# A hybrid encoder on one core: another opening, bias-first adaLN sums and another order of the mixers

## The chip, the core and the metric

The kernel runs on one of the eight cores of a Trainium2 chip. The metric is the device time of one execution in microseconds (us); the time given is the median of a few runs. Names in the profile: PE is TensorE (PEld its weight loads), DVE is VectorE, ACT is ScalarE, POOL is GpSimd, SP is the engine whose queue issues nearly all DMA transfers.

## The reference

Two layers on x (1 x 256 x 1024, float32), with a vector c (1024) that modulates both sub-layers (adaLN):

```python
c_act = silu(c)
for l in range(2):
    sh1, sc1, gt1, sh2, sc2, gt2 = split(c_act @ w_ada[l] + b_ada[l], 6)
    h = rms(x, g_mix[l]) * (1.0 + sc1) + sh1
    parts = split(h @ w_in[l], ...)          # q, k, v of A; q, k, v of three groups B; two gates
    y_a = gqa_attention(rope(rms(qa)), rope(rms(ka)), va) @ w_branch_a[l]
    y_b = dilated_attention(...) @ w_branch_b[l]      # windows (128,1), (512,4), (2048,16)
    x = x + gt1 * ((sigmoid(gate_a) * y_a + sigmoid(gate_b) * y_b) @ w_out[l])
    h2 = rms(x, g_mlp[l]) * (1.0 + sc2) + sh2
    x = x + gt2 * (square(relu(h2 @ w_ff1[l])) @ w_ff2[l])
```

## The kernel before

The 256 tokens are two tiles (t = 0, 1) of 128 partitions. Products with weights run on TensorE in three passes of a 32-bit format: a weight tile (128 x 1024, one DMA of 512 KB into one of seven buffers `wr`) is split into a high part `w[:, 0]` by ScalarE and the rest `w[:, 1]` by VectorE, and the activations hT likewise; hi x hi, lo x hi and hi x lo are summed in PSUM.

**adaLN.** c_act is broadcast to all partitions. Each of 96 tiles of w_ada is loaded through a `wr` buffer too, and VectorE multiplies it with c_act and sums along the row in one instruction (`ada_tile`; CUSTOM_DVE in the profile). Its output is one column of `shg` (shift and scale) or `gcol` (gate). The bias `b_col` and the gain `g_col` come in afterwards: `first_sh_sc` for the first mixer, one k tile at a time, `sh_sc` for the three other norms, `gt_row` for the gates.

**The opening** is written out by hand in a table `OPEN`. `loads` is the order of the first DMAs on SP's queue, behind that of c: x0 (the first token tile, with an identity of 128 columns, biases, gains and rotary constants in front, 1552 columns), x1 (1280 columns), two tiles of w_ada, then w_x and w_y of k tile 0. `steps` is the order in which the work is recorded: C is the tanh of c and the products that broadcast it (`step_c`, 128 rows of c_in of which 8 hold c), T0 and T1 the first rotary table by products on 64 rows, X0 and X1 the mean square, rstd (GpSimd, a power of -0.5), scaling, transposes by the identity and copies to xT (`step_x`), A the two reduces that give shift and scale of k tile 0 (`step_a`), H0 and H1 h = xT * scale + shift (`step_h`), W the split of the weights, M the first products, F a few products that only keep the array busy. `eng` names the engine of each step (a is ScalarE, d VectorE). The products with w_y of k tile 0 are plain float32 (`plain`). Then come k tiles 1 to 7 of the first projections, 24 products each, each with two w_ada tiles and two weight tiles of its own.

**The order.** Everything is recorded in a `Plan` before it is issued. The planner runs the recorded work against its own table of costs, picks for each engine the next instruction by due time and by what is ready, and then issues all in the order that comes out. `seq0` and `seq1` give the order in which the pieces of the two mixers are recorded (a and b are pieces of the two attentions, c2 to c5 chunks of q, k, v, u and v gate products, y the A branch, w one w_ada tile), `ada_f0` how many w_ada tiles stand between the MLP's pieces. In the trace all recorded instructions carry one line, 721, of `issue`.

The attention uses the array divided: `ka,qa` on 64 rows, `qk` in 64 x 64, `pTa,v` and `pTb,v` in 64 columns; all else uses 128 x 128.

Of the kernel before, what the change touches and what calls it, by code (L numbers as in the profile page):

```python
# [12 lines left out]
F32 = mybir.dt.float32  # L13
# [7 lines left out]
P = 128  # L21
D = 1024
# [14 lines left out]
  ada_f0=[2, 3, 11, 2, 0, 1, 0, 8, 1], ada_f1=[1, 0, 0, 0, 0, 0, 0, 0, 0],  # L37
  seq0="w v v w a w c3 c4 a w w v w a v u a w w w w w u w w w b w b w w v w u w y w w w y w y y w".split(),
  seq1="w u w c4 v w w w w w a w u w c3 w v a a w c5 w w u w w c2 w a w y w y y w y w w u w b w w w b v w v w".split())
# [7 lines left out]
FIRST = 500.0  # L47
# [6 lines left out]
X0 = 128 + 16 + 128 + 256  # L54
OPEN = dict(
    loads="x0 x1 a0 a1 wx wy",
    steps="C T1 F0 X0 A X1 T0 F1 Wy H0 Wx H1 My0 Mx0 Mx1 My1",
    eng=dict(c0="a", c1="a", ss00="d", ss01="a", ss10="d", ss11="a", xn00="a", xn01="d", xn10="a",
             xn11="a", xT00="a", xT01="a", xT10="d", xT11="a", t00="a", t01="a", t10="a", t11="a",
             h0="d", h1="a", i0="d", i1="a"),  # L60
# [96 lines left out]
class Plan:  # L157
# [101 lines left out]
    def record(self, e, op, a, k):  # L259
        outs = [k["out"]] if "out" in k else [a[0]]  # L260
        outs += [z for z in (k.get("accum_out"),) if z is not None]
        ins = [z for z in list(a if "out" in k else a[1:]) + [v for n, v in k.items() if n not in ("out", "accum_out")] if pattern(z) is not None]
        if op == "tensor_tensor_reduce":
            outs.append(ins.pop())
        o = dict(e=e, op=op, a=a, k=k, w=[self.foot(z) for z in outs], r=[self.foot(z) for z in ins], i=len(self.ops))
        o["also"], o["then"], o["soon"] = [], None, self.soon and e == "SP"
# [22 lines left out]
    def cost(e, op, outs, ins, k):  # L289
# [18 lines left out]
        if e == "SP":  # L308
# [26 lines left out]
    def links(self):  # L335
        last = {}
        for o in self.ops:
            need = {}

            def wait(j, how, o=o, need=need):  # L340
                if j != o["i"]:
                    need[j] = max(need.get(j, 0), how)

            for kind, fs in (("r", o["r"]), ("w", o["w"])):
                for name, space, p0, p1, m in fs:
                    for j, jk, q0, q1, jm in last.get(name, ()):
# [7 lines left out]
                        late = not same or o["e"] == "SP" or (o["e"] != "PE" and kind == "r")  # L354
# [46 lines left out]
    def due(self, seq, at=None):  # L401
# [12 lines left out]
        for o in reversed(self.ops):  # L414
            i = o["i"]
            d = due[i]
            lat = 3500 if o["e"] == "SP" else o["lat"]
# [12 lines left out]
    def run(self, due):  # L430
# [8 lines left out]
        free["SP"] = 0.0  # L439
        pipe = [0.0]  # L440
        dve_port, held_port, last_cut = 0.0, (0.0, 0.0), ""
        chain, pending = False, None
# [34 lines left out]
        def expect(i, depth=0):  # L477
            z = 0.0
            for j, how in ops[i]["need"].items():
                if ops[j]["e"] == "SP":  # L480
                    z = max(z, landed.get(j, 1e18))
                    continue
# [63 lines left out]
        while count < n:  # L546
            moved = False
            for e in ORDERED:
# [15 lines left out]
                if pick is None and seen[e] == state[0] and e not in again:  # L564
                    if e == "DVE" and pending is not None:
# [70 lines left out]
                if e == "DVE":  # L636
# [4 lines left out]
                    chain = o["port"] and slow == 0.0 and "reduce" not in o["op"]  # L641
                elif e == "POOL":
                    if dve_port > t + 70.0:
                        late = True
                    elif o["port"]:
                        held_port = t, t + 70.0 + 2.14 * (o["occ"] - 140.0) / 2.16
# [78 lines left out]
def encoder(ctx: ExitStack, tc: tile.TileContext, a: dict, out: bass.AP):  # L725
# [23 lines left out]

    xin = cp.tile([P, X0 + 2 * D + 256], F32, name="xin")  # L750
    x = xin[:, X0 : X0 + 2 * D].rearrange("p (t d) -> p t d", t=2)
    ident, small, gc = xin[:, :P], xin[:, P : 2 * P], xin[:, 2 * P : 2 * P + 8]
    cs_of = xin[:, 2 * P + 16 : X0], xin[:, X0 + 2 * D :]
# [17 lines left out]
    def ada_tile(l, w, s, k, col):  # L771
# [5 lines left out]
        dve.tensor_tensor_reduce(junk, raw, c_act, 0.5, 0.0, ALU.mult, ALU.add, col)  # L777

    def sh_sc(l, w, k0, k1):

        v = shg[l, w]
        dve.tensor_tensor(v[:, :, k0:k1], v[:, :, k0:k1], b_col[:, l, w, 0:2, k0:k1], op=ALU.add)
        dve.scalar_tensor_tensor(
            v[:, 1, k0:k1], v[:, 1, k0:k1], 1.0, g_col[:, l, w, k0:k1], op0=ALU.add, op1=ALU.mult
        )

    def first_sh_sc(k):

        v, gb = shg[0, 0], b_col[:, 0, 0, 1, :]
        if k == 0:  # L790
            dve.scalar_tensor_tensor(gb, gb, 1.0, g_col[:, 0, 0, :], op0=ALU.add, op1=ALU.mult)
        sc, sh = v[:, 1, k : k + 1], v[:, 0, k : k + 1]
        dve.tensor_scalar(sc, sc, g_col[:, 0, 0, k : k + 1], gb[:, k : k + 1], op0=ALU.mult, op1=ALU.add)
        dve.tensor_tensor(sh, sh, b_col[:, 0, 0, 0, k : k + 1], op=ALU.add)
# [795 lines left out]
    with plan.first():  # L1590
        sp.dma_start(c_in, a["c"])
# [41 lines left out]
    def step_c():  # L1633
# [106 lines left out]
    for k in range(1, KT):  # L1740
# [16 lines left out]
        if k == KT - 1:  # L1757
            with plan.not_before(62000.0):
# [65 lines left out]
def _layout(i):  # L1824
# [6 lines left out]
    r["c"] = con(np.concatenate([c, np.zeros((P - KT, P + KT), np.float32)], 0))  # L1831
# [13 lines left out]
    r["x0"] = con(np.concatenate([np.eye(P, dtype=np.float32), b_col, g, g0, g0, cs[0], x[0]], 1))  # L1845
    r["x1"] = con(np.concatenate([x[1], cs[1]], 1))
# [38 lines left out]
```

## Time and profile before

| | |
|---|---|
| time before, median of 3 runs | 724.83 us (724.77 to 724.99) |
| the profiled execution | 725.12 us, of which the span is 723.3 us |
| TensorE busy | 718.4 us, 99% of the span |
| VectorE, ScalarE, GpSimd busy | 587.6, 466.3, 69.6 us |
| DMA | 180.95 MB, mean 250 GB/s; over 400 GB/s from 7 to 50 us |
| granted TensorE clock | 1.0 |
| first product with a weight tile | at 12.70 us |

A row of the timeline reads: start (us), length (us), engine, line, operation, output <- inputs, shape, count, and in brackets the idle time of the engine ahead of it and what ended it. PEld rows show when the weights of a product were loaded into the array, and so the pace of TensorE. In a row of windows stand: from:to, length, busy time (count), granted clock, DMA share, GB/s. In a row of DMA issues: KB of one.

### The profile page before, as it was taken

Reading aid. Unit: us, or ns where it says so; the run is one execution under the profiler, and the core shown is the slowest. Engines: PE = TensorE matmul, PEld = TensorE weight load, DVE = VectorE, ACT = ScalarE, POOL = GpSimd, SP = SyncE. Lnnn points to the kernel's source line nnn. Section 1 sums busy time; section 2 is a strip of 40 time slices with the busy share of each in tenths; the row PEclk is TensorE's granted clock in tenths of the full one; section 3 lists DMA queues with packets and bytes.
Section 4 is the critical chain, followed back from the end, with each engine's and each line's share of the span. In section 5 each row is a group of like instructions: output and inputs, shape, how many; then the busy total and the mean of one; then the engine's idle time right before and its main releaser. Section 6 shows DMA issues by size and latency. Waiting matters only on the chain.

```text
span 723.3 us, 10610 instructions
## 1 busy us (share of the span) xinstructions
PE 718.4 (99%) x3860; PEld 597.2 (83%) x3860; DVE 587.6 (81%) x919; ACT 466.3 (64%) x791; POOL 69.6 (10%) x60
## 2 busy tenths in 40 slices
PE   9999999999999999999999999999999999999998
PEld 6788888788888888888888888878788888888887
DVE  6999999999999986594799999797899755456643
ACT  7569678965764766653565598658848766545640
POOL 0007640000100040000032201010000000000000
PEclk9999999999999999999999999999999999999999
DMA  9998668997499997596565687967376965576101
GB/s 349 408 401 270 193 203 295 348 373 243 142 350 406 381 359 278 183 325 233 175 221 207 213 328 269 338 226 280 122 258 199 344 207 159 172 229 211 52 0 59
DMA packets 50868, 180.95 MB, mean 250 GB/s; under 512 B 5728, under 2 KB 6784, under 8 KB 50816
## 3 DMA queue, kind: packets, MB, share of 16 engines
q1 hardware_dynamic: 50816, 180.28, 70.7%
q8 instruction: 30, 0.49, 0.3%
q14 instruction: 22, 0.18, 0.1%
HBM read 178.66 MB, written 1.06 MB: 248 GB/s over the span
## 4 chain that ended last, share of the span: by engine, by line
PE 98%; DMA 1%; SPq 0%; issue 0%; DVE 0%
PE ps L721 98%; DMA wr<-in_w_y 1%; SPq L721 0%; DVE xin L721 0%
## 5 line engine op out<-in xcount | busy, mean ns | idle before, releaser
L721 DVE TENSOR_TENSOR w<-wr,w 128x1024 fp32r<-128x1024 f32 x234 | 282.3, 1229 | 44.7 <-ACT w L721 44.3
L721 ACT ACTIVATE w<-wr 128x1024 fp32r<-128x1024 f32 x234 | 241.5, 1056 | 81.8 <-PE ps L721 38.9
L721 PE MATMUL ps<-w,hT 128*128 128x512 f32 x1032 | 246.4, 395 | 0.0
L721 PEld LDWEIGHTS ps<-w,hT 128*128 128x128 f32 x1032 | 190.3, 188 | 41.5 <-DVE hT L721 1.7
L721 PE MATMUL ps<-w,hid 128*128 128x512 f32 (+1 forms) x780 | 176.0, 385 | 0.0
L721 PEld LDWEIGHTS ps<-w,hid 128*128 128x128 f32 x780 | 143.1, 188 | 28.3
L721 PE MATMUL ps<-hT,w 128*128 128x512 f32 (+1 forms) x896 | 158.5, 337 | 0.0
L721 PEld LDWEIGHTS ps<-hT,w 128*128 128x128 f32 x896 | 139.4, 190 | 18.7
L721 DVE CUSTOM_DVE_ANT_0 s2k<-wr,c_act 128x1024 bf16<-128x1024 f32 x96 | 116.1, 1227 | 0.0
L721 ACT ACTIVATE s2k<-ps 128x256 f32<-128x256 f32 (+3 forms) x108 | 45.4, 440 | 81.0 <-PE ps L721 75.3
L721 DVE TENSOR_TENSOR s2k<-ps,s2k 128x256 f32<-128x256 f32 x56 | 22.8, 419 | 32.5 <-ACT s2k L721 32.5
L721 PE MATMUL ps<-w,mT 128*128 128x512 f32 x192 | 45.6, 393 | 0.0
L721 ACT ACTIVATE s2k<-s2k 128x512 f32<-128x512 f32 (+1 forms) x62 | 38.6, 623 | 9.2 <-DVE s2k L721 8.3
L721 PEld LDWEIGHTS ps<-w,mT 128*128 128x128 f32 x192 | 35.5, 188 | 7.4 <-ACT mT L721 0.2
L721 POOL TENSOR_TENSOR rstd<-rstd,half 128x8 f32<-128x8 f32 (+1 forms) x20 | 30.1, 1509 | 87.8 <-DVE rstd L721 87.7
L721 POOL TENSOR_TENSOR ss<-ss,half 128x1 f32<-128x1 f32 x8 | 11.1, 1383 | 261.7 <-DVE ss L721 254.6
L721 DVE TENSOR_TENSOR hid<-s2k,hid 128x512 fp32r<-128x512 f32 x28 | 20.1, 719 | 19.8 <-ACT hid L721 19.7
L721 ACT ACTIVATE pr<-pr,st 128x256 f32<-128x256 f32 (+1 forms) x64 | 32.3, 558 | 0.8 <-DVE st L721 0.8
L721 DVE TENSOR_TENSOR s2k<-ps,gtb 128x512 f32<-128x512 f32 (+1 forms) x18 | 11.7, 658 | 18.4 <-PE ps L721 18.4
L721 PEld LDWEIGHTS ps<-xin,s2k 128*128 128x128 f32 x180 | 20.9, 141 | 6.3 <-DVE s2k L721 1.2
L721 PE MATMUL ps<-xin,s2k 128*128 128x128 f32 x180 | 26.0, 274 | 0.0
L721 POOL TENSOR_TENSOR s2k<-s2k,tabs 128x256 f32<-128x256 f32 (+1 forms) x20 | 20.2, 1031 | 57.8 <-ACT s2k L721 51.5
(109 smaller groups left out, 505.0 us busy)
## 6 DMA issues: line engine op xcount, KB each, us to landing
wr<-in_w_ff SPq DMA_DIRECT2D x120, 512.0 KB, 4.9
wr<-in_w_ada SPq DMA_DIRECT2D x96, 512.0 KB, 5.7
wr<-in_w_gate SPq DMA_DIRECT2D x32, 512.0 KB, 4.8
wr<-in_w_qkv SPq DMA_DIRECT2D x24, 512.0 KB, 5.3
wr<-in_w_x SPq DMA_DIRECT2D x16, 512.0 KB, 5.2
wr<-in_w_out SPq DMA_DIRECT2D x16, 512.0 KB, 5.3
wr<-in_w_y SPq DMA_DIRECT2D x8, 512.0 KB, 6.7
wr<-in_w_ba SPq DMA_DIRECT2D x8, 512.0 KB, 6.1
```

Source lines behind the costliest of these rows:

```text
L721: getattr(self.real[o["e"]], o["op"])(*map(real, o["a"]), **{n: real(z) for n, z in o["k"].items()})
```

## The change

- c goes out on ScalarE's DMA queue, as 16 rows (8.5 KB) and not 128 (68 KB); its broadcast products use 16 rows of the array.
- x0 is the first DMA on SP's queue and holds x alone (512 KB); x1 holds the second tile, the biases and gains that the first norm needs (`early`), and all rotary constants (788 KB). w_y of k tile 0 comes ahead of w_x.
- The identity is made by GpSimd (a memset and a select). The other biases and gains (`small`) come in a DMA of their own near 50 us.
- A sum of adaLN begins with its bias, or is scaled by its gain, as scalar operands of the reduce (`ends`); behind it only one add is left (`one_more`, and one for each of the other norms). `gain_first` prepares the gain and (1 + bias) * gain once. `first_sh_sc`, `sh_sc` and the add in `gt_row` go.
- The opening's steps, their engines, `ada_f0`, `seq0` and `seq1` are other lists. [...]

```diff
   hk=2,
-  ada_f0=[2, 3, 11, 2, 0, 1, 0, 8, 1], ada_f1=[1, 0, 0, 0, 0, 0, 0, 0, 0],
-  seq0="w v v w a w c3 c4 a w w v w a v u a w w w w w u w w w b w b w w v w u w y w w w y w y y w".split(),
+  ada_f0=[2, 5, 7, 2, 0, 2, 0, 7, 3], ada_f1=[1, 0, 0, 0, 0, 0, 0, 0, 0],
+  seq0="w v w v a w c4 c3 w a v w w u a a w w v w u w w w b w b w w w w v w y u w w w y w w y y w".split(),
...
-    loads="x0 x1 a0 a1 wx wy",
-    steps="C T1 F0 X0 A X1 T0 F1 Wy H0 Wx H1 My0 Mx0 Mx1 My1",
...
+    loads="x0 x1 a0 a1 wy wx",
+    steps="C F0 X0 X1 T0 A Wx H0 My0 H1 Wy T1 F1 My1 Mx0 Mx1",
...
+    early = xin[:, 2 * D : 2 * D + 24].rearrange("p (s k) -> p s k", s=3)
...
+    ident = cp.tile([P, P], F32, name="ident")
+    pool.memset(ident, 0.0)
+    pool.affine_select(
+        out=ident, in_=ident, compare_op=ALU.not_equal, fill=1.0, base=0, pattern=[[-1, P]], channel_multiplier=1
+    )
...
-        dve.tensor_tensor_reduce(junk, raw, c_act, 0.5, 0.0, ALU.mult, ALU.add, col)
...
+        dve.tensor_tensor_reduce(junk, raw, c_act, *ends(l, w, s, k), ALU.mult, ALU.add, col)
+
+    def ends(l, w, s, k):
+
+        ks = slice(k, k + 1)
+        if s < 2 and (l, w) == (0, 0):
+            return (0.5, early[:, 0, ks]) if s == 0 else (early[:, 2, ks], 0.0)
+        return (g_col[:, l, w, ks], 0.0) if s == 1 else (0.5, b_col[:, l, w, s, ks])
+
+    def one_more(k):
+        sc = shg[0, 0][:, 1, k : k + 1]
+        dve.tensor_tensor(sc, sc, early[:, 1, k : k + 1], op=ALU.add)
+
+    def gain_first(g, b):
+        dve.scalar_tensor_tensor(b, b, 1.0, g, op0=ALU.add, op1=ALU.mult)
+        dve.tensor_scalar(g, g, 0.5, None, op0=ALU.mult)
...
-        sp.dma_start(c_in, a["c"])
+        act.dma_start(c_in[: 2 * KT], a["c"])
...
-            sp.dma_start(xin[:, : X0 + D], a["x0"])
+            sp.dma_start(xin[:, :D], a["x0"])
...
-            sp.dma_start(xin[:, X0 + D :], a["x1"])
+            sp.dma_start(xin[:, D:], a["x1"])
...
+            with plan.not_before(50000.0):
+                sp.dma_start(small, a["small"])
+            gain_first(g_col, b_col[:, :, :, 1, :])
```

What the planner makes of it, at two places. First VectorE in the opening, from the first reduce of w_ada with c_act (ISA; the short ISA row behind it stores the sum) to the split of w_x (`w20wx`). `shg` are the shift and scale, `xT` the transposed x, `s2k<-xT,shg` is h of one token tile, `hT` its parts. Before:

```order
L721 ISA s2k_93,shg_80<-wr_83,c_act 128x1024
L721 ISA shg_80 128x1
L721 ISA s2k_94,shg_80<-wr_84,c_act 128x1024
L721 ISA shg_80 128x1
L721 TENSOR_TENSOR shg_80<-shg_80,xin 128x1
L721 TENSOR_SCALAR shg_80<-shg_80,xin 128x1
L721 TENSOR_SCALAR s2k_98<-xT,shg_80 128x128
L721 COPY xT<-ps_74 128x4x128
L721 CAST hT_91<-s2k_98 128x128
L721 TENSOR_TENSOR hT_91<-s2k_98,hT_91 128x128
L721 TENSOR_TENSOR w20wx<-wr_85,w20wx 128x1024
```

VectorE in the same stretch of the changed kernel:

```order
L722 ISA s2k_101,shg_82<-wr_86,c_act,xin 128x1024
L722 ISA shg_82 128x1
L722 COPY xT<-ps_78 128x4x128
L722 TENSOR_TENSOR shg_82<-shg_82,xin 128x1
L722 TENSOR_SCALAR s2k_99<-xT,shg_82 128x128
L722 COPY xT<-ps_76 128x4x128
L722 CAST hT_93<-s2k_99 128x128
L722 TENSOR_SCALAR s2k_102<-xT,shg_82 128x128
L722 TENSOR_TENSOR hT_93<-s2k_99,hT_93 128x128
L722 CAST hT_93<-s2k_102 128x128
L722 ISA s2k_96,shg_82<-wr_89,c_act,xin 128x1024
```

VectorE now makes two copies to xT and h of both token tiles (ScalarE made one copy and h of the second tile before), and a reduce of k tile 1 stands ahead of the split of w_x, which follows behind the last row; of shift and scale only one add is left.

Second TensorE in the mixer of layer 0, at the attentions' divided products (`qk` on 64 x 64, `pTa,v` on 64 columns; `w,hT` are ordinary products, `pr` and `gcol` transposes). Before:

```order
L721 MATMUL ps_73<-qk_123 64x64
L721 MATMUL ps_77<-qk_123 64x64
L721 MATMUL ps_76<-pTa_0_141,v_126 64x256 x8
L721 MATMUL ps_78<-pTa_1_162,v_126 64x256 x8
L721 MATMUL ps_79<-qk_122 64x256
L721 MATMUL ps_75<-qk_122 64x256
```

TensorE there in the changed kernel:

```order
L722 MATMUL ps_81<-qk_125 64x64
L722 MATMUL ps_80<-qk_125 64x64
L722 MATMUL ps_78<-w_169,hT_93 128x512 x4
L722 MATMUL ps_76<-w_169,hT_93 128x512 x4
L722 MATMUL ps_78<-w_170,hT_93 128x512 x6
L722 MATMUL ps_76<-w_170,hT_93 128x512 x6
```

The first `qk` group is followed by ordinary products. Further on, TensorE around the `pTa,v` group of the changed kernel:

```order
L722 MATMUL ps_78<-w_172,hT_94 128x512 x4
L722 MATMUL ps_74<-pTa_0_143,v_128 64x256 x8
L722 MATMUL ps_77<-pTa_1_166,v_128 64x256 x8
L722 MATMUL ps_76<-w_172,hT_94 128x512 x6
L722 MATMUL ps_75<-qk_124 64x256
L722 MATMUL ps_81<-qk_124 64x256
```

The three groups of divided products followed each other; now ordinary products stand between each two. On the queues SP begins with x0 and x1 (c was ahead of them), and ScalarE's first instruction is the DMA of c, ahead of its table load.

More of the change, by code (lines that the diff above doesn't have):

```diff
@@ L36 @@
   hk=2,
-  ada_f0=[2, 3, 11, 2, 0, 1, 0, 8, 1], ada_f1=[1, 0, 0, 0, 0, 0, 0, 0, 0],
-  seq0="w v v w a w c3 c4 a w w v w a v u a w w w w w u w w w b w b w w v w u w y w w w y w y y w".split(),
-  seq1="w u w c4 v w w w w w a w u w c3 w v a a w c5 w w u w w c2 w a w y w y y w y w w u w b w w w b v w v w".split())
+  ada_f0=[2, 5, 7, 2, 0, 2, 0, 7, 3], ada_f1=[1, 0, 0, 0, 0, 0, 0, 0, 0],
+  seq0="w v w v a w c4 c3 w a v w w u a a w w v w u w w w b w b w w w w v w y u w w w y w w y y w".split(),
+  seq1="w u w c4 w v w w w a w u w c3 w w w v a w a w u w w c5 c2 a w w y y w w w w w y y u b w b w v v w w w".split())
 WR = 7
@@ L46 @@
 BEGIN = 20000.0
-FIRST = 500.0
+FIRST = 0.0
 LATE = 1000.0
@@ L265, in record @@
         o = dict(e=e, op=op, a=a, k=k, w=[self.foot(z) for z in outs], r=[self.foot(z) for z in ins], i=len(self.ops))
-        o["also"], o["then"], o["soon"] = [], None, self.soon and e == "SP"
+        o["dma"] = op == "dma_start"
+        o["also"], o["then"], o["soon"] = [], None, self.soon and o["dma"]
         o["from"] = self.earliest
@@ L307, in cost @@
             return occ, occ + 205
-        if e == "SP":
+        if outs and ins and op == "dma_start":
             size = max(free(z) * mybir.dt.size(z.dtype) * z.ap[0][1] for z in outs)
@@ L353, in links @@
                                 continue
-                        late = not same or o["e"] == "SP" or (o["e"] != "PE" and kind == "r")
+                        late = not same or self.ops[j]["dma"] or o["e"] == "SP" or (o["e"] != "PE" and kind == "r")
                         wait(j, 2 if late else 1)
@@ L416, in due @@
             d = due[i]
-            lat = 3500 if o["e"] == "SP" else o["lat"]
+            lat = 3500 if o["dma"] else o["lat"]
             for j, how in o["next"]:
@@ L438, in run @@
         free = dict.fromkeys(ORDERED, FROM)
-        free["SP"] = 0.0
+        free["SP"] = free["ACT"] = 0.0
         pipe = [0.0]
         dve_port, held_port, last_cut = 0.0, (0.0, 0.0), ""
-        chain, pending = False, None
+        chain, pending, last_dve = False, None, 0.0
         users = {name: len(u) for name, u in self.use.items()}
@@ L479, in expect @@
             for j, how in ops[i]["need"].items():
-                if ops[j]["e"] == "SP":
+                if ops[j]["dma"]:
                     z = max(z, landed.get(j, 1e18))
@@ L547, in run @@
             moved = False
+            if pending is not None and t >= pending[1] + 70.0 and dve_port <= pending[1] + 70.0:
+                held_port = enter(*pending, pending[1] + 70.0)
+                pending = None
             for e in ORDERED:
@@ L564, in run @@
                 if pick is None and seen[e] == state[0] and e not in again:
-                    if e == "DVE" and pending is not None:
+                    if e == "DVE" and pending is not None and t >= pending[1] + 70.0:
                         held_port = enter(*pending, t)
@@ L614, in run @@
                     heapq.heappush(q, h)
-                if e == "DVE" and pending is not None and (
+                if e == "DVE" and pending is not None and t >= pending[1] + 70.0 and (
                     pick is None or not chain or not ops[pick]["port"] or ops[pick]["occ"] < 100.0 or t > free[e] + 30.0
+                    or ops[pending[0]]["port"] or ops[pick]["occ"] < 1000.0 < last_dve
                 ):
@@ L641, in run @@
                     chain = o["port"] and slow == 0.0 and "reduce" not in o["op"]
+                    last_dve = o["occ"]
                 elif e == "POOL":
[L643 to L646, printed above, removed]
+                    late = True
+                    heapq.heappush(ev, (t + 70.0, 0, -1))
                 free[e] = 1e18 if late else t + o["occ"] + slow
                 count += 1
-                if e == "SP":
-                    quiet = t < 4000.0
+                if o["dma"]:
                     b = max(pipe[0], t + (1200.0 if t < 4000.0 else 2100.0)) + o["lat"] / RATE[t < 50000.0]
                     pipe[0] = b
-                    end = b + (1200.0 - FIRST if t < 100.0 else 1700.0) + (FIRST if t < 4000.0 else SOON if b + 1700.0 < FETCH else FETCHED if t < 45000.0 else LATE)
+                    end = b + (1200.0 - FIRST if t < 100.0 and e == "ACT" else 1700.0) + (FIRST if t < 4000.0 else SOON if b + 1700.0 < FETCH else FETCHED if t < 45000.0 else LATE)
                     landed[pick] = end
@@ L747, in f32 @@
         return t.bitcast(F32)
[L750 to L753, printed above, removed]
+    xin = cp.tile([P, 2 * D + X0 + 512], F32, name="xin")
+    x = xin[:, : 2 * D].rearrange("p (t d) -> p t d", t=2)
+    early = xin[:, 2 * D : 2 * D + 24].rearrange("p (s k) -> p s k", s=3)
+    gc = xin[:, 2 * D + 24 : 2 * D + 32]
+    cs_of = xin[:, 2 * D + X0 : 2 * D + X0 + 256], xin[:, 2 * D + X0 + 256 :]
+    small = cp.tile([P, P], F32, name="small")
+    ident = cp.tile([P, P], F32, name="ident")
[3 more added lines that the diff above has]
+    )
     c_act = cp.tile([P, D], F32, name="c_act")
@@ L776, in ada_tile @@
         junk = s2k(f"aj{i}", BF16, 1024)
-        dve.tensor_tensor_reduce(junk, raw, c_act, 0.5, 0.0, ALU.mult, ALU.add, col)
[L779 to L794, printed above, removed]
+        dve.tensor_tensor_reduce(junk, raw, c_act, *ends(l, w, s, k), ALU.mult, ALU.add, col)
[10 more added lines that the diff above has]
+        dve.tensor_scalar(g, g, 0.5, None, op0=ALU.mult)
     gcol = {}
@@ L800, in gt_row @@
         c = gcol[l, w]
-        dve.tensor_tensor(c, c, b_col[:, l, w, 2, :], op=ALU.add)
         ps = pt(f"gt{l}{w}")
@@ L820, in ada_jobs @@
                 for k in range((l, w) == (0, 0), KT):
-                    for s in range(2):
+                    for s in (1, 0) if (l, w) == (0, 0) else (0, 1):
                         ada_tile(l, w, s, k, shg[l, w][:, s, k : k + 1])
-                        if s == 1 and (l, w) == (0, 0):
-                            first_sh_sc(k)
+                        if s == 0 and (l, w) == (0, 0):
+                            one_more(k)
                         if s == 1 and k == KT - 1 and (l, w) != (0, 0):
-                            sh_sc(l, w, 0, KT)
+                            sc = shg[l, w][:, 1]
+                            dve.tensor_tensor(sc, sc, b_col[:, l, w, 1, :], op=ALU.add)
                         yield
@@ L1642, in step_c @@
                 pe.matmul(
-                    ps[:, k * P : (k + 1) * P], pick[:, kk : kk + 1].to_broadcast([P, P]), c_row,
+                    ps[:, k * P : (k + 1) * P], pick[: 2 * KT, kk : kk + 1].to_broadcast([2 * KT, P]), c_row[: 2 * KT],
                     start=True, stop=True,
@@ L1648, in step_a @@
     def step_a():
+        gain_first(early[:, 2], early[:, 1])
         for s, raw in enumerate(loaded):
             junk = s2k(f"aj0{s}", BF16, 1024)
-            dve.tensor_tensor_reduce(junk, raw, c_act, 0.5, 0.0, ALU.mult, ALU.add, v0[:, s, :1])
-        first_sh_sc(0)
+            dve.tensor_tensor_reduce(junk, raw, c_act, *ends(0, 0, s, 0), ALU.mult, ALU.add, v0[:, s, :1])
+        one_more(0)
     def step_w(n):
@@ L1830, in _layout @@
     c = np.concatenate([f["c"].reshape(KT, P), np.eye(KT, dtype=np.float32)], 1)
-    r["c"] = con(np.concatenate([c, np.zeros((P - KT, P + KT), np.float32)], 0))
+    r["c"] = con(np.concatenate([c, np.zeros((KT, P + KT), np.float32)], 0))
     b = f["b_ada"].reshape(2, 2, 3, KT, P)
@@ L1844, in _layout @@
     cs = [cs_t[:, :, t * P : (t + 1) * P].reshape(P, 256) for t in range(2)]
-    r["x0"] = con(np.concatenate([np.eye(P, dtype=np.float32), b_col, g, g0, g0, cs[0], x[0]], 1))
-    r["x1"] = con(np.concatenate([x[1], cs[1]], 1))
+    r["small"] = con(np.concatenate([b_col, g], 1))
+    r["x0"] = con(x[0])
+    r["x1"] = con(np.concatenate([x[1], b_col[:, :16], g[:, :8], g0, g0, cs[0], cs[1]], 1))
     cc = _chunk_cols()
```

6 lines of the change are left out of this document (2 added, 4 removed).

## The prediction

> **What bounds the kernel now.** I read the page first, then the chain of waits in order of time, then the weight loads of TensorE (PEld), because their starts show the pace of TensorE, which its pipelined matmul records hide.
>
> ```profile
> PE 718.4 (99%) x3860; PEld 597.2 (83%) x3860; DVE 587.6 (81%) x919; ACT 466.3 (64%) x791; POOL 69.6 (10%) x60
> 4.06 8.51 DMA wr<-in_w_y
> 12.70 18.07 PE ps L721 x71
> 30.81 689.44 PE ps L721 x3732
> ...
> 212.04 10.76 PEld L721 LDWEIGHTS ps<-w,hid 128*128 128x128 f32 x48
> ```
>
> The chain is two things: 12.6 us until the first product with a weight tile, and TensorE without a real break to 720.25. In the MLP 48 loads take 10.76 us to the end of the last, which is 0.19 long: (10.76 - 0.19) / 47 = 0.225 us each, with nothing lost. So only two kinds of stretch can move: the opening, and the two mixers, where the order of the products changes. For the opening I read what the weight loads waited for, and how full the DMA engines were.
>
> ```profile
> 19.12 0.19 PEld L721 LDWEIGHTS ps<-w,hT 128*128 128x128 f32 x1 [0.41 <-DVE hT L721]
> 30.80 4.66 PEld L721 LDWEIGHTS ps<-w,hT 128*128 128x128 f32 x21 [0.47 <-DVE hT L721]
> 35.73 0.30 PEld L721 LDWEIGHTS ps<-w,hT 128*128 128x128 f32 x2 [0.27 <-ACT hT L721]
> 36.19 5.10 PEld L721 LDWEIGHTS ps<-w,hT 128*128 128x128 f32 x23 [0.16 <-DVE hT L721]
> 41.52 15.98 PEld L721 LDWEIGHTS ps<-w,hT 128*128 128x128 f32 x71 [0.23 <-DVE hT L721]
> ...
> 28.10 1.06 ACT L721 ACTIVATE w<-wr 128x1024 fp32r<-128x1024 f32 x1 [3.21 <-DMA wr<-in_w_x]
> 18.55:41.50 22.95, 22.91 (x99) 1.00 1.03 408
> ```
>
> The last column of the last row is GB/s: until 41.5 us the 16 DMA engines are full (share 1.03, 408 GB/s). TensorE catches up with the stream at the third k tile: the x weights land at 28.10, and 2.70 us later (split on ScalarE, rest on VectorE, then the low part of hT) comes the product at 30.80. From 30.80 to 41.52 there are 21 + 2 + 23 = 46 loads, 10.35 us at 0.225; 10.72 passed, so 0.37 us more was waited. After 41.52 TensorE is its own limit.
>
> **The change, part by part.** The stream first.
>
> ```profile
> 0.74 0.38 SPq L721 DMA_DIRECT2D c_in<-in_c  x1
> 1.18 0.89 SPq L721 DMA_DIRECT2D xin<-in_x  x2
> 5.88 0.63 ACT L721 ACTIVATE s2k<-xin 128x512 bf16<-128x512 f32 x1 [2.98 <-DMA xin<-in_x]
> xin<-in_x SPq DMA_DIRECT2D x1, 776.0 KB
> xin<-in_x SPq DMA_DIRECT2D x1, 640.0 KB
> ```
>
> x0 is issued where c was, 1.18 - 0.74 = 0.44 us sooner. x0 and x1 were 1416 KB and are 512 + 788 = 1300 KB (788 from 128 x 1576 floats): 116 KB, 0.29 us at 408 GB/s. So everything after x1 lands 0.73 us sooner, if the slots of the weight buffers come free in time. They should: the tenth load behind x1 is the first to wait for work after the opening's two reduces, for a reduce that I place to end at 14.8, and the 1300 KB and nine loads of 512 KB ahead of it keep the engines busy for 14.8 us, to about 17. x0 itself saves 264 KB, 0.66 us, and 0.44: it lands at 4.8, and x1, 0.73 us sooner than by the old sizes (5.88 + 1.61), at 6.8.
>
> ```profile
> 2.59 0.31 ACT L721 ACTIVATE s2k<-c_in 8x128 f32<-8x128 f32 x1 [0.57 <-DMA c_in<-in_c]
> ...
> 3.75 3.30 PE L721 MATMUL ps<-c_in 128*128 128x128 f32 x16
> ...
> 7.62 2.01 PE L721 MATMUL ps<-s2k,xin 64*128 64x128 f32 x16
> ...
> L721 POOL TENSOR_TENSOR s2k<-s2k,tabs 128x256 f32<-128x256 f32 (+1 forms) x20 | 20.2, 1031 | 57.8 <-ACT s2k L721 51.5
> ```
>
> c (8.5 KB) goes out on ScalarE's queue ahead of its table load. ScalarE idled 0.57 us before the tanh, and the issue takes 0.38 as it did on SP: nothing. The c products take 16 rows of the array, not 128. The nearest row, products on 64 rows, takes 2.01 us for twice the columns, so half of 3.30; the bounds are a quarter of 3.30 and all of it. c_act is needed only by the reduces at 8.6, and even 3.30 ends at 7: nothing.
>
> The identity is a memset and a select of 128 columns on GpSimd. Its products of 256 columns average 1.03 us, so from the engines' start at 0.8 it is there at 2.8 by that, and at half of it at 1.8. Its first reader on VectorE stands just ahead of c's product, which needs the tanh (2.9). Cost 0; with 1 us more, c_act would be ready about when the reduces need it.
>
> The chain that sets k tile 1 is VectorE's. Before:
>
> ```profile
> 8.99 1.22 DVE L721 CUSTOM_DVE_ANT_0 s2k<-wr,c_act 128x1024 bf16<-128x1024 f32 x1
> ...
> 10.14 1.22 DVE L721 CUSTOM_DVE_ANT_0 s2k<-wr,c_act 128x1024 bf16<-128x1024 f32 x1
> ...
> 11.28 0.15 DVE L721 TENSOR_TENSOR shg<-shg,xin 128x1 f32<-128x1 f32 x1
> 11.40 0.27 DVE L721 TENSOR_SCALAR shg<-shg,xin 128x1 f32<-128x1 f32 x1
> 11.78 0.35 DVE L721 TENSOR_SCALAR s2k<-xT,shg 128x128 f32<-128x128 f32 x1
> 12.04 0.68 DVE L721 COPY xT<-ps 128x512 f32<-128x512 f32 x1
> 12.64 0.21 DVE L721 CAST hT<-s2k 128x128 fp32r<-128x128 f32 x1
> ...
> 17.87 0.58 ACT L721 ACTIVATE hT<-xT,shg 128x256 fp32r<-128x256 f32 x1
> 18.65 0.42 DVE L721 TENSOR_TENSOR hT<-s2k,hT 128x256 fp32r<-128x256 f32 x1
> ```
>
> Start to start a reduce takes 1.15, the copy 0.60. New order: x0's sum 4.8 to 5.5, its small step and rstd by GpSimd (half of 1.57, the first row of rival 2) to 6.4, scaling 0.4 (to 8.99 from 8.59 before), x1's sum and the diagonal (0.6 each) and four small steps with their waits to 8.6; two reduces to 10.85; copy 11.45; one add 0.15 in place of 0.15 + 0.27; h of half 0 at 11.7. Its y product starts at 12.1 instead of 12.70, and the wait for w_y is gone, since w_y is now the fifth load. Then a copy (0.60), cast (0.21), h of half 1 (0.26 to the next start, as 11.78 to 12.04), the low part of half 0 and another cast (0.21 each): 13.5. Two reduces and the rest of w_x (3 x 1.14): 16.9; low part and add: 17.25. ScalarE's h and hi (0.49 + 0.58) end at 18.35, VectorE's low part at 18.8, and the product that stood at 19.12 starts at 18.9. VectorE has one copy, one h and one cast more there (some 1.1 us), which eats most of its earlier start.
>
> From 18.9 some 50 products lead to the one at 30.80: 18.9 + 50 x 0.225 = 30.15. By the stream it can start at 30.80 - 0.73 = 30.07. So 0.65 is won there. Later tiles:
>
> ```profile
> 34.09 0.15 DVE L721 TENSOR_TENSOR shg<-shg,xin 128x1 f32<-128x1 f32 x1
> 34.21 0.27 DVE L721 TENSOR_SCALAR shg<-shg,xin 128x1 f32<-128x1 f32 x1
> ```
>
> With the bias inside the sum the 0.39 from the first start to the second end becomes 0.15, so the low part of k tile 4 is 0.73 + 0.24 earlier and TensorE no longer waits for it: most of the 0.37 is won too. **Opening: -0.9 us** (ends 0 and -1.2: nothing if VectorE's chain is as late as before, everything if it hides fully). The same bias steps in the three other adaLN rows and the gates lie beside a full TensorE: 0. The 64 KB of constants go out near 50 us; whoever needs them comes after 55, and TensorE is 10 products ahead of them: 0 (a late landing would cost up to 0.5).
>
> The mixers' order. In layer 0 VectorE and ScalarE only cover TensorE; what counts is how often the array changes its division.
>
> ```profile
> 123.86 0.76 PEld L721 LDWEIGHTS ps<-qk 64*64 64x64 f32 x24 [0.17 <-issue]
> ...
> 128.29 2.09 PEld L721 LDWEIGHTS ps<-qk 64*64 64x64 f32 x72 [0.38 <-issue]
> ...
> 472.48 3.22 PEld L721 LDWEIGHTS ps<-pTa,v 128*64 128x64 f32 x32 [0.35 <-ACT s2k L721]
> 492.10 2.75 PEld L721 LDWEIGHTS ps<-qk 64*64 64x64 f32 x96 [0.35 <-ACT G L721]
> ```
>
> Before, the three groups of layer 0 follow each other: 0.17 + 0.38 idle. Now ordinary products stand between them, so each is entered as in layer 1, at 0.35: 1.05, that is **+0.5 us**. Bursts of transposes: one more in layer 0, one fewer in layer 1: 0. Other waits of the mixers may appear or go; I take 0 for them, with -0.8 and +0.5 as ends (all idle of the weight loads after 42 us beyond these entries is about 0.8).
>
> Sum: -0.9 + 0.5 = -0.4 us. The profiled execution is 725.12 us for its span of 723.3; it would be 724.7. Its median of three runs is 0.29 lower, 724.83, so I predict **724.4**.
>
> **Rivals.**
>
> 1. The new order of the mixers also saves waits: -0.9, and -0.6 of those 0.8, the entries being hidden: 723.3. For it speaks that idle of 0.2 to 0.4 us stands at many places; against it, that the MLP and most mixer stretches already run at 0.225.
>
> 2. GpSimd's rstd of x1 gets stuck, and the kernel is slower.
>
> ```profile
> 7.54 1.57 POOL L721 TENSOR_TENSOR ss<-ss,half 128x1 f32<-128x1 f32 x2 [7.10 <-DVE xin L721]
> ...
> 372.00 3.48 DVE L721 TENSOR_TENSOR w<-wr,w 128x1024 fp32r<-128x1024 f32 x3
> 372.15 4.87 POOL L721 TENSOR_TENSOR ss<-ss,half 128x1 f32<-128x1 f32 x1 [13.19 <-DVE ss L721]
> 375.40 1.21 DVE L721 CUSTOM_DVE_ANT_0 s2k<-wr,c_act 128x1024 bf16<-128x1024 f32 x1
> ```
>
> The same step took 4.87 us at 372.15, until VectorE's chain of four ended at 376.61. In the new order it is asked for some 0.1 us before the two reduces begin. Stuck to their end (10.85 + 0.4), x1's scaling (two of 0.65) and transposes end at 13.1, VectorE's second copy waits 1.1 us, k tile 1 starts at 20.0, and TensorE is at 20.0 + 96 x 0.225 = 41.6 where it was at 41.52: +0.1, with the mixers +0.6: 725.4. It decides from about 0.9 us of delay upward. [...]
>
> [...]
>
> 4. The stream doesn't come earlier, since the first 3 us are start-up and not bytes: opening 0, 725.3. Against it: x0 lands 4.70 us after its issue, of which 776 KB are 1.95 at full rate; the rest goes with the issue.
>
> **How the numbers follow.** Forecast 0.45; rivals 0.2, 0.1, 0.15, 0.1. The forecast's own range is 723.9 to 724.9. To hold 8 in 10 it takes in most of rivals 1 to 4: 723.2 to 725.5. About 0.2%, 1.45 us, is what a measurement of this kernel can tell from no change: faster means below 723.38, a little more than half of rival 1 (0.13); slower means above 726.28, beyond every case here, left with 0.04; the same 0.83.
>
> **What would show it.** Right: ScalarE's first wait for x ends near 4.8; the first product with w_y near 12.1 without a wait for its DMA; the product of 19.12 at 18.9, that of 41.52 at 40.6; the three entries in layer 0 with 0.35 each; everything from 205 to 340 shifted by one amount. Wrong: GpSimd's second step longer than 1 us; a gap in the DMA rate between 14 and 25 us; a constant that arrives after its reader; more than 0.5 us of new idle ahead of weight loads between 60 and 200 us.

## The result, and the profile after

The changed kernel takes 729.29 us (median of 6 runs, 728.52 to 730.08), the kernel before 724.85 (6 runs beside them): a ratio of 1.0060, 95% interval 1.0047 to 1.0073. Forecast were 724.4 us and a range up to 725.5; it is 4.4 us slower than the kernel before and 4.9 above the forecast. The profiled execution is the slowest of the six, 730.08 us for a span of 728.3.

The timeline of TensorE (PE) and ScalarE in the opening of the changed kernel, rows as in the prediction:

```profile
0.73 0.41 ACTq L722 DMA_DIRECT2D c_in<-in_c  x1
3.59 0.31 ACT L722 ACTIVATE s2k<-c_in 8x128 f32<-8x128 f32 x1 [1.13 <-DMA c_in<-in_c]
4.54 0.63 ACT L722 ACTIVATE s2k<-xin 128x512 bf16<-128x512 f32 x1 [0.64 <-DMA xin<-in_x]
...
1.45 2.50 PE L722 MATMUL ps<-warm 128*128 128x512 f32 x4 [1.45 <-DVE half L722]
4.26 3.78 PE L722 MATMUL ps<-c_in 16*128 16x128 f32 x16 [0.31 <-DVE c_in L722]
7.97 1.65 PE L722 MATMUL ps<-warm 128*128 128x384 f32 x2
9.41 1.91 PE L722 MATMUL ps<-ident,s2k 128*128 128x128 f32 x8
11.26 3.38 PE L722 MATMUL ps<-s2k,xin 64*128 64x128 f32 x16
```

x0 is there at 4.5 us, even sooner than forecast. But c, issued at 0.73 as before at 0.74, is there at 3.59, not 2.59. And TensorE runs at half pace: two warm products of 384 columns take 1.65 us (0.81 before), the 16 rotary products 3.38 (2.01 before). The trace's record of the granted clock says the same: full from 14.09 us on, in the kernel before from 6.57. (The clock column of a stretch shows 1.00 all the same, since the record only begins there.)

What that starts is seen on VectorE (DVE), on SyncE's queue (SPq) and in the DMA rate. The rows of the last three are of the windows: length, busy times of five engines, granted clock, DMA share, GB/s.

```profile
12.23 0.35 DVE L722 TENSOR_SCALAR s2k<-xT,shg 128x128 f32<-128x128 f32 x1
15.26 0.69 DVE L722 COPY xT<-ps 128x512 f32<-128x512 f32 x1 [2.68 <-PE ps L722]
...
16.36 1.02 PE L722 MATMUL ps<-wr,s2k 128*128 128x512 f32 x2
16.59 1.28 DVE L722 CUSTOM_DVE_ANT_0 s2k<-wr,c_act,xin 128x1024 bf16<-128x1024 f32 x1
...
11.24 7.00 SPq L722 DMA_DIRECT2D wr<-in_w_ada  x2
...
5.00:15.00 10.00, 10.00 (x45) 7.47 (x44) 6.29 (x18) 5.80 (x13) 1.10 (x2) 1.00 1.02 412
15.00:20.00 5.00, 5.00 (x18) 2.59 (x16) 4.74 (x9) 3.24 (x5) 0.00 (x0) 1.00 0.68 246
20.00:50.00 30.00, 30.00 (x134) 24.80 (x133) 29.07 (x47) 17.59 (x23) 0.00 (x0) 1.00 1.01 391
```

VectorE stands 2.68 us for TensorE's transposes, the first y product starts at 16.36 in place of 12.70, the reduce that frees a buffer ends at 17.9, and SyncE waits for that buffer: the stream that I had 0.73 us ahead has a hole between 15 and 20 us.

To see where the 5.0 us between the two profiled executions arise, I put TensorE of both in step by work: each product counts with the median distance of its form to the next, warm-up products are left out, and the lag is how much later the other kernel has done the same work. It is 3.5 us at 20 us, 2.9 at 50, 3.1 at 100, 4.1 at 130, 4.7 from 200 to 480 and 4.9 at the end. So 2.9 us belong to the opening, 1.8 to the mixer of layer 0 and 0.2 to that of layer 1. In the MLP nothing is lost (PEld are weight loads; before 212.04 and also 10.76):

```profile
216.75 10.76 PEld L722 LDWEIGHTS ps<-w,hid 128*128 128x128 f32 x48
```

In the mixer of layer 0 these are the breaks around the divided products, and in the groups of instructions the reduce has a new price:

```profile
115.22 0.76 PEld L722 LDWEIGHTS ps<-qk 64*64 64x64 f32 x24 [0.36 <-issue]
...
122.65 2.38 PEld L722 LDWEIGHTS ps<-w,hT 128*128 128x128 f32 x11 [0.38 <-DVE w L722]
...
127.19 3.22 PEld L722 LDWEIGHTS ps<-pTa,v 128*64 128x64 f32 x32 [0.36 <-issue]
130.80 1.23 PEld L722 LDWEIGHTS ps<-w,hT 128*128 128x128 f32 x6 [0.38 <-issue]
132.38 2.09 PEld L722 LDWEIGHTS ps<-qk 64*64 64x64 f32 x72 [0.36 <-issue]
...
L722 DVE CUSTOM_DVE_ANT_0 s2k<-wr,c_act,small 128x1024 bf16<-128x1024 f32 x80 | 101.8, 1282 | 8.4 <-DMA wr<-in_w_ada 8.4
```

### The profile page after: what moved, and what is told of

It reads as the page before. It is cut to its first block, busy times and chain, and to the rows that moved or that the text cites. A ratio compares the mean times of both kernels' runs of the same rounds, so it can differ in the third digit from the quotient of the medians.

```text
span 728.3 us, 10596 instructions
## 1 busy us (share of the span) xinstructions
PE 723.3 (99%) x3860; PEld 599.3 (82%) x3860; DVE 593.6 (82%) x910; ACT 466.1 (64%) x788; POOL 71.7 (10%) x62
## 4 chain that ended last, share of the span: by engine, by line
PE 96%; DVE 2%; ACT 1%; issue 1%; DMA 0%; DVEq 0%
PE ps L722 96%; DVE s2k L722 1%; DVE w L722 0%; DMA c_in<-in_c 0%; DVE st L722 0%; ACT pr L722 0%; ACT w L722 0%; DVE rstd L722 0%; ACT qk L722 0%; DVE xin L722 0%; ACT s2k L722 0%; DVE c_in L722 0%; DVE gcol L722 0%; DVEq L722 0%
## 5 line engine op out<-in xcount | busy, mean ns | idle before, releaser
L722 DVE CUSTOM_DVE_ANT_0 s2k<-wr,c_act,small 128x1024 bf16<-128x1024 f32 x80 | 101.8, 1282 | 8.4 <-DMA wr<-in_w_ada 8.4
L722 POOL TENSOR_TENSOR rstd<-rstd,half 128x8 f32<-128x8 f32 (+1 forms) x20 | 32.0, 1605 | 142.0 <-DVE rstd L722 141.8
L722 POOL TENSOR_TENSOR ss<-ss,half 128x1 f32<-128x1 f32 x8 | 9.4, 1181 | 262.6 <-DVE ss L722 260.3
L722 PEld LDWEIGHTS ps<-ident,s2k 128*128 128x128 f32 x180 | 21.5, 145 | 7.6 <-DVE s2k L722 2.0
L722 PE MATMUL ps<-ident,s2k 128*128 128x128 f32 x180 | 27.1, 282 | 0.0
L722 PE MATMUL ps<-w,oa 128*128 128x512 f32 x96 | 23.2, 393 | 0.0
```

What stands on the lines that cost most here:

```text
L722: getattr(self.real[o["e"]], o["op"])(*map(real, o["a"]), **{n: real(z) for n, z in o["k"].items()})
```

## The experiments

Each ran on one chip in a row with the kernel before. "Full clock" is where the trace's record of the granted clock begins to be full; the lags are TensorE's against the kernel before, as above. Both are of the one profiled execution of each kernel, the medians are of all its runs. The planner, whose own table of costs the change alters too, computes the order anew for each kernel, so that an edit in the opening can move rows of the mixers; where it did not, I say so.

| kernel | full clock at | lag at 50 us | lag at 230 us | median (kernel before beside it) |
|---|---|---|---|---|
| before | 6.57 | 0 | 0 | 724.85 |
| changed | 14.09 | 2.87 | 4.71 | 729.29 (724.85) |
| c_first | 13.50 | 2.63 | 4.77 | 728.86 (724.90) |
| c_128 | 11.23 | 2.10 | 3.42 | 728.64 (724.90) |
| c_pad | 9.55 | 0.91 | 3.89 | 728.27 (725.00) |
| c_both | 5.50 | -0.71 | 0.71 | 726.37 (725.14) |
| warm13 | 7.40 | 1.73 | 4.65 | 729.77 (725.14) |
| b_16 | 13.13 | 2.43 | 2.44 | 727.24 (725.14) |
| b_32 | 13.38 | 2.53 | 2.58 | 727.13 (725.00) |
| b_64 | 11.49 | 1.81 | 1.83 | 727.06 (725.00) |
| sums_old | 12.69 | 2.81 | 4.26 | 729.39 (724.90) |
| seq_old | 13.50 | 2.65 | 5.53 | 730.76 (724.90) |
| both_sums | 5.83 | -0.44 | 1.40 | 726.46 (725.14) |
| both_seq | 5.12 | -0.74 | 2.10 | 728.04 (725.02) |
| both_old | 5.42 | -0.05 | 1.91 | 727.16 (725.02) |
| b_col | 4.34 | -0.07 | 1.02 | 726.82 (725.02) |
| b_seq | 4.49 | -0.37 | 1.17 | 726.70 (725.02) |

**The opening: lateness or rows of c?** First each of the two edits on c undone alone.

c_first:

```diff
-        act.dma_start(c_in[: 2 * KT], a["c"])
+        sp.dma_start(c_in[: 2 * KT], a["c"])
```

> The changed kernel with one edit: the 16 rows of c go out as SyncE's first load, ahead of x0, not on ScalarE's queue. In the changed kernel c landed at 3.57 us (2.56 before), TensorE stood from 3.95 to 4.26, and its products ran at the slow pace (16 rotary products in 3.38 us, 2.01 before) until 14.1 us (6.6 before). Theory P (the late c made TensorE pause, and the pause put off its full clock): c lands near 2.6, the two warm products of 384 columns take 0.8 and the rotary products 2.0 us again, full clock near 6.6; of the 3 us that TensorE was behind at 50 us some 2.5 to 3.5 come back: 725.8 to 726.8. Theory R (it is the products on 16 rows that do not bring the full clock, whenever they come): rotary products still near 3.4 us, full clock after 10 us, only the second or so of c's lateness can come back: 728.3 to 729.3.

728.86 us, and full clock at 13.50 us. TensorE's pause is gone, and yet the pace stays low:

```profile
1.45 2.50 PE L722 MATMUL ps<-warm 128*128 128x512 f32 x4 [1.45 <-DVE half L722]
3.88 3.78 PE L722 MATMUL ps<-c_in 16*128 16x128 f32 x16
7.59 1.65 PE L722 MATMUL ps<-warm 128*128 128x384 f32 x2
9.03 1.92 PE L722 MATMUL ps<-ident,s2k 128*128 128x128 f32 x8
10.88 3.27 PE L722 MATMUL ps<-s2k,xin 64*128 64x128 f32 x16
```

Theory P, with which I had begun, falls: TensorE works without a pause from 1.45 us and is not given its full clock before 13.50.

c_128:

```diff
-        act.dma_start(c_in[: 2 * KT], a["c"])
+        act.dma_start(c_in, a["c"])
-                    ps[:, k * P : (k + 1) * P], pick[: 2 * KT, kk : kk + 1].to_broadcast([2 * KT, P]), c_row[: 2 * KT],
+                    ps[:, k * P : (k + 1) * P], pick[:, kk : kk + 1].to_broadcast([P, P]), c_row,
```

> The changed kernel with one edit: c as 128 rows again (the rows beyond 8 zero), still on ScalarE's queue, and its products on 128 rows of the array. Theory P (the pause of TensorE while c is late sets the clock): c still lands near 3.6, TensorE still pauses, the rotary products still take 3.4 us: 729.0 to 729.6. Theory R (products on 16 rows do not bring the full clock): c's products bring it by about 8 us, the rotary products take 2.0, 2 to 3 us come back: 726.2 to 727.3.

728.64: between the two theories. With c's 68 KB on ScalarE's queue and x0 as SyncE's first load, ScalarE could read c only at 4.55 (at 2.69 in c_both below, where c is SyncE's first load), and TensorE stood 1.27 us, longer than I had expected (0.31 in the changed kernel). Full clock came 6.0 us after c's products began. The two edits hide each other, so the next kernel undid both.

c_both:

```diff
-        act.dma_start(c_in[: 2 * KT], a["c"])
+        sp.dma_start(c_in, a["c"])
```
(and the products on 128 rows as in c_128)

> The changed kernel with c as before in both respects: 128 rows, first load on SyncE's queue, products on 128 rows of the array; all else as changed. With c early but on 16 rows full clock came at 13.5 us, with c late but on 128 rows at 11.2 us. [...] Rival N (something else in the new opening, such as the order of transposes and rotary products, keeps the clock low): full clock after 10 us, 728 to 729.5.

726.37 us, 2.9 less than the changed kernel; its ratio to before is 1.0018 (1.0009 to 1.0027). By theory R+ (theory R, and products on 128 rows from 1.45 us on bring the clock) I had put 725.2 to 727.0. Full clock came at 5.50 us; that such products must run for a fixed time no run shows.

```profile
3.75 2.79 PE L722 MATMUL ps<-c_in 128*128 128x128 f32 x16
6.38 0.81 PE L722 MATMUL ps<-warm 128*128 128x384 f32 x2
7.02 1.04 PE L722 MATMUL ps<-ident,s2k 128*128 128x128 f32 x8
8.34 2.01 PE L722 MATMUL ps<-s2k,xin 64*128 64x128 f32 x16 [0.28 <-DVE s2k L722]
...
12.31 3.67 PE L722 MATMUL ps<-wr,s2k 128*128 128x512 f32 x8
...
19.06 25.94 PEld L722 LDWEIGHTS ps<-w,hT 128*128 128x128 f32 x115 [0.27 <-DVE hT L722]
```

These kernels can be compared with each other: TensorE, VectorE and GpSimd have the same order in c_first, c_128 and c_both. With c early the 16 rows, loaded and used, cost 2.5 us (728.86 against 726.37); with c on 128 rows its place on ScalarE's queue costs 2.3 (728.64 against 726.37). Either edit alone costs nearly as much as both.

b_16, the same question asked of the kernel before, with the order unchanged on every engine:

```diff
-                    ps[:, k * P : (k + 1) * P], pick[:, kk : kk + 1].to_broadcast([P, P]), c_row,
+                    ps[:, k * P : (k + 1) * P], pick[: 2 * KT, kk : kk + 1].to_broadcast([2 * KT, P]), c_row[: 2 * KT],
```

> The kernel before with one edit and the same instruction order on every engine: c's 16 products read 16 rows (16 rows of the array), not 128; the load is unchanged. Theory R+: they do not bring the full clock, which opens after 10 us in place of 6.6; rotary products slow, 1.5 to 3.5 us lost in the opening: 726.4 to 728.5. Rival N: nothing changes, 724.6 to 725.1. By my forecast for this term (c's products get shorter): at most 725.0 and c's products under 3.3 us.

727.24 us, ratio 1.0030 (1.0020 to 1.0039): this line alone costs 2.1 us (runs from 726.55 to 727.89).

```profile
3.88 3.78 PE L721 MATMUL ps<-c_in 16*128 16x128 f32 x16
7.59 1.65 PE L721 MATMUL ps<-warm 128*128 128x384 f32 x2
9.17 3.79 PE L721 MATMUL ps<-s2k,xin 64*128 64x128 f32 x16
```

The lag is 2.4 us from 40 us to the end: a late opening by itself costs the mixers nothing there. For b_64 and b_32 the `2 * KT` above reads 64 and 32.

> The kernel before, c's products on 64 rows of the array (order the same on every engine but for one swap of two neighbours on ScalarE). If rows count in proportion with a threshold of half or below: full clock by 7 us, 724.7 to 725.4. If 64 rows are too few as 16 are: full clock after 10 us, 726.5 to 727.9.

> The kernel before, c's products on 32 rows of the array, order the same on every engine. If 32 rows are too few as 16 are: full clock after 10 us, 726.5 to 727.9. If 32 rows do: by 7 us, 724.7 to 725.4.

727.06 and 727.13: on half the rows of the array c's products cost the kernel as much as on an eighth.

c_pad leaves c where the change put it (32 rows of it) and widens the products:

```diff
+    act.dma_start(c_in[: 4 * KT], a["c"])
+    pool.memset(c_in[32:64], 0.0)
+    pool.memset(c_in[64:128], 0.0)
```
(and the products on 128 rows as in c_128)

> The changed kernel, c still on ScalarE's queue and about as late (32 rows are loaded, the other 96 are set to zero by GpSimd), but its 16 products on 128 rows of the array. [...] If the lateness alone decides: clock after 12.5 us, 729 to 730.

Full clock at 9.55, 5.1 us after c's products began at 4.49; the lag at 50 us is 0.91: with the wide products, though c is late, 2.0 of the opening's 2.9 us come back. Behind it this kernel lost 3.0 us by 230 us, 1.0 of it already between 50 and 60, in an order that the planner had made anew: 728.27, with runs from 726.62 to 729.35.

warm13 (`WARM = 5` to `WARM = 13`) brings the clock with other products:

> The changed kernel with one edit: 13 in place of 5 units of warm-up products on 128 rows (0.43 us each at the slow clock), so that TensorE has products on 128 rows from 1.45 to about 7 us; c stays late and on 16 rows. Theory R+: full clock between 5 and 7.5 us, c's products behind it in about 1.8 us; c_act is there 0.5 to 1 us later than in the changed kernel (8.7), yet the transposes and rotary products take half: TensorE at 50 us 1 to 2.5 us nearer to before, 726.5 to 728.3. Rival N: full clock after 10 us, c_act 2 us later: 730 to 732.

Full clock at 7.40, as expected, c's products in 2.08 us where I had put about 1.8, and the lag at 50 us 1.1 smaller. Yet 729.77: the new order lost 2.9 us between 50 and 230 us. The bound that I gave for the sum left that out and missed.

**The mixers: sums or lists?** sums_old has `0.5, 0.0` again for `*ends(...)`, and `first_sh_sc` and the steps on bias and gain behind the reduce; seq_old has `ada_f0`, `seq0`, `seq1` of before.

> The changed kernel with the adaLN sums as before: constants 0.5 and 0 as the operands of the reduce, the bias and gain steps behind it. In the changed kernel a reduce with a column operand takes 1.28 us, before 1.22, and there are 96. Theory S (the dearer reduce makes VectorE the bound in the mixer of layer 0, where TensorE loses 1.3 us against before between 100 and 125 us): reduces at 1.22 again, 1.0 to 1.8 us come back: 727.5 to 728.3. Theory O (the new order of the mixers loses it): 728.9 to 729.8. Either way the opening stays late.

> The changed kernel with the two mixers' order lists and the list of adaLN jobs of before. Theory O (the new order loses the 1.3 us between 100 and 125 us and the 0.6 later): 1.2 to 1.9 us come back: 727.4 to 728.1. Theory S (the dearer reduce loses it): 728.9 to 729.8. By my forecast's term for the order (three entries at 0.35 and nothing else) 0.5 comes back: 728.8.

729.39 and 730.76: neither gives anything back. The first lies in theory O's range, the second above every range that I had given: the old lists in the changed kernel are 1.5 us worse than the new ones. The same edits on c_both, where the opening is on time (both_sums has the first, both_seq the second, both_old both):

> The kernel c_both with the adaLN sums as before too (constants as operands of the reduce, the bias and gain steps behind). Theory S (with TensorE on time, what is left is VectorE, which does not wait between 60 and 150 us, so that each 0.06 us of a reduce counts there): 0.7 to 1.5 us less than c_both. Rival (VectorE's late start was all): the same as c_both within 0.4 us.

> The kernel c_both with the order lists of before, sums as changed. Theory A (lists of before are the better ones): 725.0 to 726.2. Theory L (they fit only the old program, as seq_old showed): 727.0 to 729.0.

> The kernel c_both with the adaLN sums as before and the order lists of before: what is left of the change is x ahead of the constants, the identity by GpSimd, the new order of the opening's steps. c_both gained 0.7 us in the opening (TensorE at 50 us) and lost 1.6 behind it. Theory A (the sums and lists together lose the 1.6): the mixers go as before, 724.1 to 724.9 beside 725.1 for the kernel before. Theory L (an order list fits only the program that it was made for: the old lists in the changed kernel lost 3.4 us between 50 and 720 us): 726 to 728.

726.46, 728.04 and 727.16 beside 726.37 of c_both. Theory L holds for the two kernels with old lists. In both_sums theory S got nothing. And both_old, which has neither the lists nor the sums of the change, still falls back by 2.0 us between 50 and 230 us. So the single edits on the kernel before, first the lists alone (`seq0`, `seq1`, `ada_f0`):

> The kernel before with the new order lists and list of adaLN jobs alone. Theory O (the new lists lose what c_both lost behind the opening): 1.2 to 1.7 us slower, 726.3 to 726.8. Theory L (new lists in the old program fit badly, worse than in their own): 727 to 729. By my forecast for this term, +0.5: 725.6.

726.70, as theory O had it: 1.7 us. Then the operand alone, with the same order on every engine:

```diff
-        dve.tensor_tensor_reduce(junk, raw, c_act, 0.5, 0.0, ALU.mult, ALU.add, col)
+        dve.tensor_tensor_reduce(junk, raw, c_act, 0.5, zero, ALU.mult, ALU.add, col)
```

> The kernel before, with the zero that each adaLN reduce takes as its start given as a column (a tile of zeros) and not as a constant; bias and gain steps stay, and so does the order of the instructions on every engine. It prices the operand alone. The 96 reduces should go from 1.22 to 1.28 us. Theory V (VectorE hardly waits between 60 and 150 us, so the 20 or so reduces there delay TensorE): 0.4 to 1.3 us slower, 725.5 to 726.4. Rival (TensorE has lead enough over VectorE): within 0.3 us of before.

726.82, ratio 1.0027 (1.0016 to 1.0037): 1.8 us, more than I gave it. The reduce's group before and in b_col (busy, mean ns, idle), and what weight loads waited for between 60 and 240 us, first before, then b_col (us in total, times, longest):

```profile
L721 DVE CUSTOM_DVE_ANT_0 s2k<-wr,c_act 128x1024 bf16<-128x1024 f32 x96 | 116.1, 1227 | 0.0
...
PEld ps L721 <- issue: 1.4, 5, 0.4
PEld ps L721 <- DVE s2k L721: 0.7, 3, 0.3
```

```profile
L721 DVE CUSTOM_DVE_ANT_0 s2k<-wr,c_act,zero 128x1024 bf16<-128x1024 f32 x96 | 122.0, 1289 | 0.0
...
PEld ps L721 <- issue: 2.0, 6, 0.4
PEld ps L721 <- DVE s2k L721: 1.5, 4, 0.6
```

Of 96 x 0.062 = 6.0 us more work on VectorE 1.0 reaches TensorE by 230 us and another 0.7 between 430 and 510 us, in the two mixers; the rest is hidden.

## Why the prediction was wrong, step by step

- **c on ScalarE's queue: nothing** (wrong). ScalarE waited 1.13 us where it had waited 0.57, and c was there 1.0 us later (3.59, not 2.59), with x0's 512 KB issued on SyncE's queue at the same moment (0.74; in c_first, ahead of x0 on SyncE's queue, the same 8.5 KB were read at 2.35). I priced the issue on ScalarE and not when c would land. Whether x0 beside it makes c late, or ScalarE's queue by itself, was not tested. What the lateness is worth depends on the rows: with c on 16 rows c_first gives back 0.24 us by 50 us, with 128 rows the queue makes 2.3 us (c_128 against c_both).
- **c's products on 16 rows: "half of 3.30 ... even 3.30 ends at 7: nothing"** (this step failed). They took 3.78, beyond my upper bound, and their own length was not the point: c's products on 16, 32 or 64 rows did not bring TensorE's full clock (it came at 13.13, 13.38 and 11.49 us), on 128 rows they did (6.57). Two comparisons show it, b_16 forwards, with that edit alone and the order unchanged (2.1 us lost), and c_both against c_first backwards (full clock at 5.50, not 13.50; 2.5 us); c_pad, where c is late and the order made anew, agrees (9.55, not 14.09). Where products on 128 rows run from 1.45 us without a pause, the clock is full at 4.3 to 7.4 us, which is 2.9 to 5.9 us after the first of them; with narrow products until about 7.6 or 8, it is full at 11.5 to 14.1. How long products on 128 rows must run for it, the runs do not show beyond that. Most kernels of the second kind also spread more (728.52 to 730.08 here, 725.96 to 726.87 for c_both), but not all (seq_old 730.43 to 731.26).

  I had read PE rows before and after 6.6 us in the trace of before without asking why the same products get faster there. The row of 2.01 us, from which I took "half of 3.30", ran wholly at full clock, while c's products started one every 0.21 us until 6.57, at half clock, and every 0.11 behind it. And its products, on 64 rows each, start in pairs 7 ns apart, on both halves of the array: neither its time nor its rows carry over to c's products, which run one at a time. What such pairs do for the clock is not shown; they were running when it rose in five of the seven kernels with narrow products until 7.6 or 8.
- **Stream 0.73 us sooner** (right as far as it goes): x0 at 4.5, and x1's sum starts at 6.58 without a wait. But it rested on a reduce ending at 14.8 that frees a buffer; it ended at 17.9, hence the hole in the stream, a gap in the DMA rate between 14 and 25 us such as I had named as a sign of an error. This is the clock's doing too, by way of the transposes that VectorE waits 2.68 us for.
- **VectorE's chain, first y product at 12.1, product of 19.12 at 18.9** (right, under full clock): c_both has them at 12.31 and 19.06. The opening then gains 0.7 us where I said 0.9.
- **Identity by GpSimd: 0** (right): memset and select end at 1.30, sooner than my 1.8. **Rivals 2 and 3** (GpSimd's rstd of x1 held up by the reduces): it ran from 8.46 for 0.55 us, and the first reduce began at 8.71. They didn't occur, and how far a single reduce would hold this step up, the case to which I gave 0.15 as rival 3, was not tested: in this run no reduce was under way when it was asked for.
- **Reduce at unchanged 1.22** (wrong): 1.28. I took an operand's kind as free. In the order of before this is worth 1.8 us (b_col); in the changed order taking it back gained nothing (both_sums), with the bias steps back and the order made anew, so what it costs there stays open.
- **Bias inside the sum saves a step** (right in kind): with the old steps the lag at 50 us is -0.44 (both_sums), without them -0.71 (c_both). The order was made anew in between and the clock was full 0.33 us later in both_sums, so the size is not shown.
- **Mixers +0.5** (sign right, size wrong): c_both loses 1.5 us from 60 to 230 us and 0.2 in layer 1. I counted three entries at 0.35 against 0.55. The trace has four breaks of 0.36, 0.36, 0.38 and 0.36, since `pTa,v` now stands alone and the way back from it to full width costs as well (the 0.38 of before, which I had read as the entry of `qk`, also stood behind `pTa,v`): 1.46 against 0.55, +0.9. And one wait of 0.38 for a split by VectorE, where I had put 0 for "other waits", is new. These five are worth 1.3 us; between 100 and 130 us the lag grows by 1.0. b_seq shows that the lists alone cost the kernel before 1.7 us.

Summed up: forecast -0.9 and +0.5; measured on the profiled executions +2.9 and +2.0. The +2.9 comes with c's two edits and the late clock, for with early c on 128 rows the opening is -0.7. How the +2.0 of the mixers divides stays open: in the order of before the lists cost 1.7 us and the operand 1.8, but both_old loses 2.0 us in the mixer of layer 0 without either, in an order that the planner made anew. Among the signs of an error I had named "more than 0.5 us of new idle ahead of weight loads"; the larger part of the loss was no such idle, it was products at half pace in the opening, which a list of waits doesn't show.

No kernel here beats the one before: the gain of the new opening (0.7 us) is there in c_both, but each order of the mixers that went with it here gives back more. That another list would keep the 0.7 is not shown.

## What to carry to other kernels

Before making the first products narrower or later, look at where the same product changes its duration in the opening (c's here from 0.42 to 0.28 us, at 6.57), and at what runs until then. Here c's products on 16 to 64 rows did not bring the full clock (it came at 11.49 to 13.38 us in place of 6.57), and where TensorE stood 1.27 us ahead of wide ones (c_128) it came at 11.23 us, not at 5.50 (c_both). An operand's kind and a queue were not free here (0.062 us a reduce, 1.0 us for c): price them by a run with that edit alone, with the order unchanged. And when an order list was made for one program, an edit elsewhere moves it: read each stretch's lag apart, or a gain of 0.7 us is lost in a new order.

## What the runs showed of the hardware that I had not expected

- With c's products on 16, 32 or 64 rows in the first 8 us TensorE's clock is full at 13.1, 13.4 and 11.5 us, against 6.6 with 128 rows (4.3 in b_col, in the same order): about 2.1 us of the whole kernel.
- c's products of 128 columns took as long on 16 rows as on 128 (0.21 us from one record to the next at half clock, in both kernels): fewer rows saved no time.
- A column in place of a constant as the start of the multiply-and-sum on 128 x 1024: 1.289 us, not 1.227.
- A load of 8.5 KB, issued on ScalarE's queue at the same moment as 512 KB on SyncE's, was read 1.0 us later (at 3.59) than 68 KB issued 0.4 us ahead of 776 KB on SyncE's (at 2.59).
